# Two reorderings in the feed-forward part of a two-layer trunk: another PSUM bank for one transposition, and the fourth weight set made before the third

## The chip, the cores and the metric

The kernel runs on one core of a Trainium2 chip. Times are microseconds (us) on the device. Before the change three runs gave 1443.37, 1441.01 and 1440.71, so the median is 1441.01. The profiled execution is a fourth one and took 1442.07.

## The reference

The input x has 512 tokens of 1024 features, all in float32. Two layers each do this:

- `h = x + W_out( sigmoid(gA) * PoolMixer(u) + sigmoid(gB) * DiffAttn(q, k, v) )`, where one projection of `RMSNorm(x)` gives u, q, k, v, gA and gB
- `x' = h + (silu(gate) * up) @ w_ffn_out`, where `gate, up = split(RMSNorm(h) @ w_ffn_in)`, each 2816 wide

The change touches the feed-forward part: the transposition of `RMSNorm(h)` (and of the next layer's `RMSNorm(x)`), and the weights of `w_ffn_in`.

## The kernel before

**Precision.** Every matrix product in float32 is made of three passes in fp32r. Each operand is split in a rounded part (`hi`) and the rest (`lo`), and TensorE adds `hi*hi`, `hi*lo` and `lo*hi` in PSUM. `split` (lines 195, 196) makes `hi` with a ScalarE cast and `lo` with a VectorE subtraction. `parts` has a second way for weights that lie in DRAM as they are (lines 233 to 235): ScalarE casts `hi`, ScalarE writes the negated rounded value into `lo`, and a DMA issued by GpSimd adds the float32 weights from DRAM onto it. So `lo` is ready when that DMA has landed.

**Norm and transposition.** 512 tokens are 4 tiles of 128 (t = 0 to 3). `normed` scales a tile by its norm (VectorE, line 336) and later, in `turn`, TensorE transposes it: eight transposes of 128x128 (line 300), four into each of two PSUM tiles named `tr`. There are two `tr` buffers, one bank each. The result is read out by `split` for the next layer's input, or by `Quarters.put` for the feed-forward part. For t of 2 and 3, `put` makes sums and differences with the tile of two tokens before (VectorE, lines 389, 390, 395, 398) and splits each of them; both halves of a token are read until line 395. The bank `oy` holds the sums of the attention heads and isn't used outside attention.

**The feed-forward input projection.** Hidden columns are done in pairs of 128-column blocks (`Ffn`, f0 = 0, 2, 4 up to 20: eleven pairs a layer). A pair's gate and up weights and the two halves of the features make a 2x2 block product, which is done with seven products in place of eight. A product is 24 matmuls of 128x256 (`pair_product`, lines 291, 293, 294). It needs a set of weights: sets 1, 2 and 4 are weights as they are and take the DMA way, sets 3, 5, 6 and 7 are sums or differences that VectorE makes from raw weights (lines 774 to 776 and 785) and take the VectorE way. TensorE takes the products in the order 1, 6, 5, 2, 7, 3, 4; the fourth one goes into a `tr` tile. Between the products VectorE adds partial results (lines 816, 824, 830, 836): line 816 reads the accumulator of the sixth product, and the seventh product accumulates onto it and so comes after it.

**Buffers and order.** The split weights stand in six buffers for `hi` (`whi`) and six for `lo` (`wlo`), taken in turn: a set that is made sixth after another takes its buffer, and must wait for the last matmul that reads it. The raw weights have seven buffers, loaded by DMAs that SP issues. Each engine does its instructions in a fixed order that a scheduler writes when the program is built: it goes by the order of the program and by its own forecast of when each operand is there. `tc.issue_after(x)` makes what is traced in its block, on the engine of x, come after x.

In a layer the first two pairs (`early`, f0 = 0 and 2) are begun while the tokens are still normed; their `sums()` is called without `a12` and makes sets 6, 4, 5, 7, 3 in this order. Each later pair calls `sums(True)`, in which the sets are made in the order 1, 6, 5, 2, 7, 3, 4.

Of the kernel before, what the change touches and what calls it, by code (L numbers as in the profile page):

```python
# [13 lines left out]
AF = mybir.ActivationFunctionType  # L14
# [8 lines left out]
NT = S // P  # L23
# [84 lines left out]
def trunk_kernel(  # L108
# [12 lines left out]
    nc = tc.nc  # L121
# [10 lines left out]
    def tr_ps():  # L132
        return ps.tile([P, 512], F32, name="tr", tag="tr", bufs=2)

    oy = ps.tile([P, 2, VD], F32, name="oy", tag="oy")
# [12 lines left out]
    scale = const.tile([P, L * KD + KD], F32, name="scale")  # L148
# [40 lines left out]
    plan = weight_plan()  # L189
    at = [0]  # L190
    transfers = []

    def split(hi, lo, src):

        ins = nc.scalar.copy(hi, src)  # L195
        nc.vector.tensor_sub(lo, src, hi.bitcast(F32))  # L196
        return ins
# [17 lines left out]
    def loaded():  # L215

        i = at[0]
        at[0] += 1
        raw = sb.tile([P, 4, VD], F32, name="raw", tag="raw", bufs=RAWS)
        nc.sync.dma_start(raw.rearrange("p a b -> p (a b)"), wts[i])  # L220
        return i, raw

    def tiles(x):
        return [x[:, k, :] for k in range(x.shape[1])]

    def parts(src, piece_no=None):

        hi = sb.tile([P, 4, VD], F32R, name="whi", tag="whi", bufs=SPLITS)
        lo = sb.tile([P, 4, VD], F32R, name="wlo", tag="wlo", bufs=SPLITS)
        if piece_no is None:  # L230
            split(hi, lo, src)
        else:
            nc.scalar.copy(hi, src)
            nc.scalar.activation(lo, src, AF.Copy, scale=-1.0)  # L234
            nc.gpsimd.dma_start(lo.rearrange("p a b -> p (a b)"), wts[piece_no], accum_op=ALU.add)  # L235
        return tiles(hi), tiles(lo)

# [22 lines left out]
    def later(delay, what):  # L260
        heapq.heappush(waiting, (clock[0] + delay, count[0], what))
        count[0] += 1
# [36 lines left out]
    def transpose(dst, src):  # L299
        nc.tensor.transpose(dst, src, ident)  # L300
        clock[0] += 2 * P

    def rsqrt_mean(ss, n, width, times=(1.0,), eps=None):

        r = sb.tile([P, width], F32, name="r", tag="r", bufs=4)
        part = width // len(times)
        for i, f in enumerate(times):
            cs = slice(i * part, (i + 1) * part)
            e = EPS / (f * f) if eps is None else eps[i]
            nc.vector.tensor_scalar(r[:, cs], ss[:, cs], 1.0 / (n * f * f), e, op0=ALU.mult, op1=ALU.add)  # L310
        nc.gpsimd.tensor_tensor(r, r, mhalf[:, :width], op=ALU.pow)  # L311
        return r

    def small(name, width=1):
        return sb.tile([P, width], F32, name=name, tag=name, bufs=4)
# [12 lines left out]
    def normed(key, t, xh, xl, g, into=None):  # L328

        xs = sb.tile([P, D], F32, name="xs", tag="mj", bufs=2)  # L330
        ss = small("ss")
        nc.scalar.activation(xs, res[t], AF.Square, accum_out=ss)
        r = rsqrt_mean(ss, D, 1)
        for half in range(2):
            cs = slice(half * 512, (half + 1) * 512)
            nc.vector.scalar_tensor_tensor(xs[:, cs], res[t][:, cs], r, g[half], op0=ALU.mult, op1=ALU.mult)  # L336

        def turn():
            tvs = []
            for half in range(2):  # L340
                tp = tr_ps()
                for i in range(4):
                    k = half * 4 + i
                    transpose(tp[:, i * P:(i + 1) * P], xs[:, k * P:(k + 1) * P])
                tv = tp.rearrange("p (k c) -> p k c", k=4)
                tvs.append(tv)
                if into is None:
                    ks = slice(half * 4, half * 4 + 4)
                    copied = split(xh[:, ks, t * P:(t + 1) * P], xl[:, ks, t * P:(t + 1) * P], tv)
            if into is not None:  # L350
                copied = into(t, tvs)
            ready.add((key, t))
            return copied

        later(NORM_WAIT, turn)
# [158 lines left out]
    for layer in range(L):  # L514
# [197 lines left out]
        def add_out(pairs, t, cb, parts=1, store=False):  # L712
            n = 512 // parts
            for i in range(parts):
                here = mm_ps()[:, :n]
                product(here, [(a, (b[0][:, i * n:(i + 1) * n], b[1][:, i * n:(i + 1) * n])) for a, b in pairs])
                cs = slice(cb * 512 + i * n, cb * 512 + (i + 1) * n)
                added = nc.vector.tensor_add(res[t][:, cs], here, res[t][:, cs])  # L718
                if store:
                    nc.sync.dma_start(out[token(t), cs], res[t][:, cs])  # L720
            return added
# [13 lines left out]
        def hidden_pair(f0):  # L735
            tag = HIDDEN_AT[f0]
            if tag in ("u", "m", "mj"):
                hh, hl = (sb.tile([P, 2, S], F32R, name="f" + part, tag=tag, bufs=2) for part in "hl")
                return [(hh[:, i, :], hl[:, i, :]) for i in range(2)]
            tags = (("pr0", 2), ("pr1", 2)) if tag == "pr" else (("up", 2), ("us", 2))  # L740
            out = []
            for tg, bufs in tags:
                out.append([sb.tile([P, S], F32R, name="f" + part, tag=tg, bufs=bufs) for part in "hl"])
            return out

        class Ffn:
# [12 lines left out]
            def gate(self, k, piece_no=None):  # L759
                self.sets[1 + k] = parts(self.r12 if k else self.r11, piece_no)  # L760
# [4 lines left out]
            def sums(self, a12=False):  # L765

                _, r21 = loaded()
                n22, r22 = loaded()
                if a12:
                    self.gate_raw(1)  # L770
                s1 = sb.tile([P, 4, VD], F32, name="ws", tag="raw", bufs=RAWS)
                if a12:
                    self.gate(0, self.n11)
                nc.vector.tensor_add(s1, r21, r22)
                nc.vector.tensor_sub(r21, self.r11, r21)
                nc.vector.tensor_sub(self.r11, s1, self.r11)
                self.sets[6] = parts(self.r11)
                if not a12:
                    self.sets[4] = parts(r22, n22)
                self.sets[5] = parts(s1)  # L780
                if a12:
                    self.gate(1, self.n12)
                else:
                    self.sets[7] = parts(r21)
                nc.vector.tensor_sub(self.r12, self.r12, self.r11)
                if a12:
                    self.sets[7] = parts(r21)
                self.sets[3] = parts(self.r12)
                if a12:
                    self.sets[4] = parts(r22, n22)  # L790
                self.to = hidden_pair(self.f0)
                for i in range(2):
                    hidden[self.f0 + i] = self.to[i]
# [189 lines left out]
```

## Time and profile before

| what | value |
|---|---|
| median of three runs | 1441.01 us |
| profiled execution | 1442.07 us, with a span of 1440.3 us from its first to its last instruction |
| TensorE (PE) busy | 1431.5 us, 99% of the span |
| VectorE (DVE), ScalarE (ACT), GpSimd (POOL) busy | 991.1, 689.1, 115.1 us |
| granted TensorE clock | 1.000 over the whole span |

PE is busy nearly throughout, so what can change is the sum of its few stops and what each of them is waiting for. The profile models the end of a matmul, so that consecutive ones overlap on paper: how long a group takes is read from the start of its first matmul to the start of what follows it.

### The profile page before, as it was taken

The numbers are of one execution on the slowest core, as the hardware profiler recorded it, in microseconds if no ns is written. First come the engines' busy times: TensorE is split into PE (matmuls) and PEld (weight loads), VectorE is DVE, ScalarE is ACT, GpSimd is POOL, SyncE is SP. The second block draws the span as 40 slices with busy tenths as digits, with TensorE's granted clock in tenths as the row PEclk, the third lists the DMA queues.
The fourth block names the chain that finished last, engine by engine and source line by source line (L and its number), as shares of the span: only waits on it lengthen the run. The fifth ranks groups of instructions, "written<-read, shape, count | busy, mean of one in ns | idle before, by whom it ended". The sixth has DMA issues, their size and how long they took to land.

```text
span 1440.3 us, 21598 instructions
## 1 busy us (share of the span) xinstructions
PE 1431.5 (99%) x8375; PEld 1261.0 (88%) x8375; DVE 991.1 (69%) x1841; ACT 689.1 (48%) x1311; POOL 115.1 (8%) x146
## 2 busy tenths in 40 slices
PE   9999999999999999999999999999999999999999
PEld 6878888888999889989888888888889998999897
DVE  7767677677898548737676685675769975587462
ACT  6544353444667337526355443434546662464350
POOL 1010000000011001001010101001000110010000
PEclk9999999999999999999999999999999999999999
DMA  9311231224258357728322132222332783575361
GB/s 348 109 61 59 96 117 59 89 73 124 66 158 215 117 133 181 200 44 227 124 88 81 59 114 73 85 73 74 114 77 74 188 218 106 130 190 164 78 157 59
DMA packets 50070, 173.02 MB, mean 120 GB/s; under 512 B 5680, under 2 KB 6576, under 8 KB 49968
## 3 DMA queue, kind: packets, MB, share of 16 engines
q1 hardware_dynamic: 39744, 137.02, 28.5%
q0 software_dynamic: 8928, 32.51, 12.6%
q10 hardware_dynamic: 1296, 2.11, 0.6%
q8 instruction: 66, 1.08, 0.3%
q14 instruction: 36, 0.29, 0.1%
HBM read 169.52 MB, written 2.10 MB: 119 GB/s over the span
## 4 chain that ended last, share of the span: by engine, by line
PE 90%; DVE 4%; issue 3%; DMA 2%; POOL 1%; ACT 0%; SPq 0%; POOLq 0%; ACTq 0%
PE mm L279 19%; PE mm L281 19%; PE mm L280 19%; PE mm L291 5%; PE mm L293 5%; PE mm L294 5%; PE sc L294 2%; PE sc L293 2%; PE sc L291 2%; PE tr L300 2%; PE tr L294 1%; DMA wlo<-in_wts 1%; PE tr L291 1%; PE tr L293 1%; DVE xs L336 1%
## 5 line engine op out<-in xcount | busy, mean ns | idle before, releaser
L195 ACT CAST whi<-raw 128x1024 fp32r<-128x1024 f32 (+1 forms) x223 | 232.2, 1047 | 206.6 <-issue 117.2
L196 DVE TENSOR_TENSOR wlo<-raw,whi 128x1024 fp32r<-128x1024 f32 (+1 forms) x223 | 269.6, 1216 | 78.0 <-ACT whi L195 75.0
L279 PE MATMUL mm<-whi,xh 128*128 128x512 f32 x480 | 192.5, 401 | 0.0
L280 PE MATMUL mm<-wlo,xh 128*128 128x512 f32 x480 | 188.0, 392 | 0.5 <-DVE wlo L196 0.5
L281 PE MATMUL mm<-whi,xl 128*128 128x512 f32 x480 | 187.8, 391 | 0.0
L718 DVE TENSOR_TENSOR res<-mm,res 128x512 f32<-128x512 f32 (+1 forms) x97 | 65.9, 683 | 116.0 <-PE mm L281 115.9
L281 PE MATMUL mm<-whi,fl 128*128 128x512 f32 (+1 forms) x358 | 138.7, 387 | 0.0
L279 PE MATMUL mm<-whi,fh 128*128 128x512 f32 (+1 forms) x358 | 138.4, 387 | 0.0
L280 PE MATMUL mm<-wlo,fh 128*128 128x512 f32 (+1 forms) x358 | 138.3, 387 | 0.0
L311 POOL TENSOR_TENSOR r<-r,mhalf 128x1 f32<-128x1 f32 (+1 forms) x76 | 58.2, 765 | 637.2 <-DVE r L310 574.3
L281 PEld LDWEIGHTS mm<-whi,xl 128*128 128x128 f32 x480 | 90.1, 188 | 19.7 <-issue 0.2
L280 PEld LDWEIGHTS mm<-wlo,xh 128*128 128x128 f32 x480 | 90.5, 188 | 17.3 <-DVE wlo L196 0.8
L279 PEld LDWEIGHTS mm<-whi,xh 128*128 128x128 f32 x480 | 90.3, 188 | 16.8
L235 POOL DMA_DIRECT2D wlo<-in_wts x62 | 54.3, 876 | 614.9 <-ACT wlo L234 263.7
L279 PE MATMUL mm<-xh,whi 128*128 128x512 f32 x256 | 102.1, 399 | 0.0
L281 PE MATMUL mm<-xh,wlo 128*128 128x512 f32 x256 | 100.0, 391 | 0.0
L291 PE MATMUL mm<-xrh,whi 128*128 128x256 f32 x352 | 99.9, 284 | 0.2
L280 PE MATMUL mm<-xl,whi 128*128 128x512 f32 x256 | 99.9, 390 | 0.0
L293 PE MATMUL mm<-xrl,whi 128*128 128x256 f32 x352 | 99.8, 284 | 0.0
L294 PE MATMUL mm<-xrh,wlo 128*128 128x256 f32 x352 | 99.8, 283 | 0.0
L291 PE MATMUL mm<-xqh,whi 128*128 128x256 f32 x352 | 99.8, 283 | 0.0
L293 PE MATMUL mm<-xql,whi 128*128 128x256 f32 x352 | 99.8, 283 | 0.0
(212 smaller groups left out, 3527.8 us busy)
## 6 DMA issues: line engine op xcount, KB each, us to landing
raw<-in_wts SPq DMA_DIRECT2D x243, 512.0 KB, 4.4
wlo<-in_wts POOLq DMA_DIRECT2D x62, 512.0 KB, 7.9
res<-in_x SPq DMA_DIRECT2D x4, 512.0 KB, 8.8
pwr<-in_pool_w ACTq DMA_DIRECT2D x8, 256.0 KB, 2.7
out<-res SPq DMA_DIRECT2D x7, 256.0 KB, 2.0
xr<-in_x_t SPq DMA_DIRECT2D x3, 512.0 KB, 8.3
g<-in_gains SPq DMA_DIRECT2D x6, 256.0 KB, 3.3
xr<-in_x_t SPq DMA_DIRECT2D x2, 256.0 KB, 4.4
```

Of the source, the lines that this page charges most:

```text
L195: ins = nc.scalar.copy(hi, src)
L196: nc.vector.tensor_sub(lo, src, hi.bitcast(F32))
L235: nc.gpsimd.dma_start(lo.rearrange("p a b -> p (a b)"), wts[piece_no], accum_op=ALU.add)
L279: nc.tensor.matmul(acc, lhsT=ah, rhs=bh, start=i == 0, stop=False)
L280: nc.tensor.matmul(acc, lhsT=ah, rhs=bl, start=False, stop=False)
L281: nc.tensor.matmul(acc, lhsT=al, rhs=bh, start=False, stop=i == n - 1)
L291: nc.tensor.matmul(acc[:, i, :], lhsT=ah, rhs=bh, start=start and not i and not k, stop=False, skip_group_check=True)
L293: nc.tensor.matmul(acc[:, i, :], lhsT=ah, rhs=bl, start=False, stop=False, skip_group_check=True)
L294: last = nc.tensor.matmul(acc[:, i, :], lhsT=al, rhs=bh, start=False, stop=i == 1 and k == 3, skip_group_check=True)
L300: nc.tensor.transpose(dst, src, ident)
L311: nc.gpsimd.tensor_tensor(r, r, mhalf[:, :width], op=ALU.pow)
L718: added = nc.vector.tensor_add(res[t][:, cs], here, res[t][:, cs])
```

## The change

The transposition of the last token tile (t = 3) puts its first half into the bank `oy` and only its second half into a `tr` tile; this holds for both norms that go through `turn`. In the pairs with `a12`, set 4 is made before set 3. In all pairs the ScalarE cast of set 3 is ordered behind the latest negating copy of `parts` (line 234).

```diff
+    negated = []
...
-            nc.scalar.activation(lo, src, AF.Copy, scale=-1.0)
+            negated[:] = [nc.scalar.activation(lo, src, AF.Copy, scale=-1.0)]
             nc.gpsimd.dma_start(lo.rearrange("p a b -> p (a b)"), wts[piece_no], accum_op=ALU.add)
...
-                tp = tr_ps()
+                tp = oy.rearrange("p a b -> p (a b)") if t == NT - 1 and not half else tr_ps()
...
                 if a12:
                     self.sets[7] = parts(r21)
-                self.sets[3] = parts(self.r12)
-                if a12:
                     self.sets[4] = parts(r22, n22)
+                with tc.issue_after(negated[-1].ins):
+                    self.sets[3] = parts(self.r12)
```

## Rows read from the trace of the kernel before

**Rows 1.** The page, part 1: busy time, share of the span, instructions.

```profile
PE 1431.5 (99%) x8375; PEld 1261.0 (88%) x8375; DVE 991.1 (69%) x1841; ACT 689.1 (48%) x1311; POOL 115.1 (8%) x146
```

**Rows 2.** PE's waits over the span: us in total, times, longest.

```profile
PE tr L294 <- DMA wlo<-in_wts: 1.2, 2, 0.7
...
PE tr L300 <- DVE xd L395: 0.9, 2, 0.6
...
PE tr L300 <- DVE xl L196: 0.2, 1, 0.2
```

**Rows 3.** PE's timeline (start, us, what), first layer: tiles t = 2, t = 3.

```profile
376.64 1.03 PE L300 MATMUL tr<-ident,xs 128*128 128x128 f32 x8
377.43 0.36 PE L291 MATMUL sc<-xqh,whi 128*128 128x256 f32 x1
...
383.32 0.60 PE L300 MATMUL tr<-ident,xs 128*128 128x128 f32 x4
...
384.90 0.36 PE L291 MATMUL sc<-xqh,wxh 128*128 128x256 f32 x1
```

**Rows 4.** Stretches: length, PE, PEld, DVE, ACT, POOL busy, clock, DMA share, GB/s.

```profile
376.30:396.30 20.00, 19.43 (x161) 19.02 (x159) 19.85 (x31) 13.18 (x21) 1.45 (x2) 1.00 0.44 122
1090.50:1110.50 20.00, 19.68 (x163) 19.22 (x161) 19.85 (x31) 13.23 (x21) 1.47 (x2) 1.00 0.47 124
```

**Rows 5.** Timelines of DVE and PE, first layer, around the sixth and seventh products.

```profile
389.69 0.69 DVE L196 TENSOR_TENSOR xrl<-xd,xrh 128x512 fp32r<-128x512 f32 x1
...
390.49 0.33 PE L293 MATMUL mm<-xrl,whi 128*128 128x256 f32 x1
...
394.43 1.22 DVE L774 TENSOR_TENSOR ws<-raw 128x1024 f32<-128x1024 f32 x1
395.57 0.69 DVE L816 TENSOR_TENSOR cqn<-mm,cqn 128x512 f32<-128x512 f32 x1
...
396.40 0.36 PE L291 MATMUL mm<-xrh,whi 128*128 128x256 f32 x1
```

**Rows 6.** PE's timeline: fourth product and what follows, both layers.

```profile
437.01 0.28 PE L291 MATMUL tr<-xth,whi 128*128 128x256 f32 x1
437.13 0.28 PE L293 MATMUL tr<-xtl,whi 128*128 128x256 f32 x1
438.08 0.39 PE L294 MATMUL tr<-xth,wlo 128*128 128x256 f32 x1 [0.66 <-DMA wlo<-in_wts]
...
440.81 0.28 PE L291 MATMUL sc<-xqh,whi 128*128 128x256 f32 x1
...
1154.82 0.28 PE L291 MATMUL sc<-xqh,whi 128*128 128x256 f32 x1
```

**Rows 7.** Timelines of ACT and POOL around the late transfers, both layers.

```profile
424.88 1.06 ACT L195 CAST whi<-raw 128x1024 fp32r<-128x1024 f32 x1 [1.07 <-DVE raw L785]
...
426.79 1.06 ACT L234 ACTIVATE wlo<-raw 128x1024 fp32r<-128x1024 f32 x1
...
428.20 0.86 POOL L235 DMA_DIRECT2D wlo<-in_wts  x1 [4.52 <-ACT wlo L234]
430.64 0.88 POOL L235 DMA_DIRECT2D wlo<-in_wts  x1 [1.57 <-ACT wlo L234]
...
1144.86 0.87 POOL L235 DMA_DIRECT2D wlo<-in_wts  x1 [1.49 <-ACT wlo L234]
```

**Rows 8.** DMA queues, 428.3:432.3: packets, MB, share of 16 engines.

```profile
q1 hardware_dynamic: 403, 1.46, 100.9%
```

**Rows 9.** Two more stretches, with the columns of rows 4.

```profile
424.00:440.50 16.50, 15.84 (x130) 15.47 (x130) 13.80 (x16) 10.57 (x12) 2.62 (x3) 1.00 0.97 253
1138.50:1154.00 15.50, 14.94 (x124) 14.68 (x123) 13.10 (x16) 10.18 (x11) 2.62 (x3) 1.00 1.03 257
```

**Rows 10.** DMA issues, 430.5:431.5, then 1144.5:1145.5: size, us to landing.

```profile
wlo<-in_wts POOLq DMA_DIRECT2D x1, 512.0 KB, 9.9
...
wlo<-in_wts POOLq DMA_DIRECT2D x1, 512.0 KB, 9.1
```

## The prediction

> **What bounds the kernel now.** I read the page first: PE is busy 1431.5 of 1440.3 us [rows 1], so the kernel is as long as PE's stream of matmuls, and only PE's stops can be won or lost. Next I read PE's list of waits [rows 2]. Three of its entries lie where the change works: two stops in the fourth product of a pair, until the accumulating DMA of its set has landed; two stops among the transposes, until VectorE has read a `tr` tile (line 395, in `put`); and one more among the transposes of the other norm. All five together are 2.3 us of idle time in a span of 1440.3. The other 20 of the 22 fourth products do not stop at all.
>
> A stop costs more than its idle time, since the matmul behind it starts with a longer step, so I price each from start to start. Eight unbroken transposes take 377.43 - 376.64 = 0.79; the last tile's eight take 384.90 - 383.32 = 1.58 [rows 3]. The stop there costs 0.79; 0.6 of it is idle [rows 2], so 0.2 is restart. The second layer's stop of this kind has the other 0.3 of the 0.9 idle and so costs 0.5, and the one of 0.2 at the other norm costs 0.4. For the fourth product: matmuls of a pair start 0.12 apart (437.13 - 437.01), 24 of them take 2.88, and this product took 440.81 - 437.01 = 3.80 [rows 6]. So this stop costs 0.92, of which 0.66 is idle and 0.26 restart. The second layer's has the remaining 0.5 to 0.6 idle of [rows 2], and costs 0.8. The whole of what the change can take away is therefore 0.79 + 0.5 + 0.4 + 0.92 + 0.8 = 3.4 us.
>
> Then I read, for each stop, what is late next: busy time by stretch [rows 4], the timelines around each place [rows 5 to 7], and the DMA queues [rows 8 to 10].
>
> **The change part by part.**
>
> *The last tile's first half goes to `oy`.* No instruction is added; four transposes write another bank. That bank's earlier users are the heads' sums of the same layer, and its next ones those of the next layer, both far from here, so I put no wait on it. The second half finds the `tr` tile that the third token freed first. All three transposition stops go.
>
> Whether this time is kept is another matter. In the 20 us from 376.3 on, VectorE is busy 19.85, and 19.85 again in the same stretch of the second layer [rows 4]. It is the engine that is late there, and the change takes no work off it. The first matmul after the stop that depends on it is the second one of the sixth product: it reads `xrl`, which VectorE finishes at 389.69 + 0.69 = 390.38, and it starts at 390.49 [rows 5]. There is 0.11 of slack. If PE arrives 0.79 earlier, it waits here. The seventh product has no slack at all: it comes after line 816, which ends at 395.57 + 0.69 = 396.26, and it starts right behind it, at 396.40. So with VectorE's order as it is, the 0.79 and 0.5 of the feed-forward norm are worth 0: the transposes end earlier and the seventh product starts when it did. The bounds are 0 and 1.29 gained (VectorE's order lets line 816 come earlier by as much); I take 0, because both layers' stretches are full.
>
> At the other norm, between the layers, PE goes on with projections of tiles that were normed before, and no wait of PE on VectorE's norm stands in [rows 2] beside this one. I take the whole 0.4 as won (bounds 0.2, the idle time alone, and 0.4).
>
> *Set 4 before set 3.* Nothing is added or removed: two ScalarE copies and one GpSimd DMA issue move ahead of one cast and one subtraction. In the pair with the late transfer ScalarE stands idle for 1.07, from 423.81 to 424.88, because the cast of set 3 waits for VectorE's line 785; only then come set 4's cast and negation, until 426.79 + 1.06 = 427.85, and the DMA is issued at 428.20, 0.35 later [rows 7]. With set 4 first, its cast can start at about 423.8. Its buffer is now the one that the previous pair's set 3 used, which PE has left by then. Cast and negation take 1.06 each, so the negation ends at about 425.9 and the DMA is issued at about 426.3, 1.9 earlier.
>
> What is that worth at landing? From its issue to PE's next matmul it took 438.08 - 428.20 = 9.9 [rows 6, 7], and that is not its own length: for the 4 us from 428.3 on the queue of the raw loads (q1) was the only one with packets, at a share of 100.9% [rows 8]. What was issued before it was served before it. Issued 1.9 earlier it has no more ahead of it than before, so with the same 9.9 at most it lands by 436.2; it is wanted at 437.13 + 0.12 = 437.25. I take both fourth-product stops as gone.
>
> What is late next is the transfer behind it, set 1 of the next pair. It was issued at 430.64 and took 9.9, so it landed at 440.5 [rows 7, 10]. PE wants it at the third matmul of the next pair: 440.81 + 0.24 = 441.05 before, 440.13 when the stop of 0.92 is gone [rows 6]. The DMA engines are busy 0.97 of the time from 424 to then [rows 9], and the same bytes are still to be moved, with this one last; so I leave its landing at 440.5. Then a new stop of 0.4 idle and 0.1 to 0.26 restart appears, and the first layer keeps 0.92 - 0.5 = 0.4. In the second layer the same transfer landed 9.1 after its issue at 1144.86, at 1153.96 [rows 7, 10]; it will be wanted at 1154.82 - 0.8 + 0.24 = 1154.26 [rows 6]. That is 0.3 of slack, and the second layer keeps all of its 0.8. Bounds for the two layers together: 0.4 (both moved to another transfer) and 1.72.
>
> The Trainium skill, "DMA: Bandwidth & Descriptors", section "Queues, rings and completion order", says that each DMA engine takes the queue rows that have work in turn, switching at packet boundaries. By that rule the accumulating queue would not have to let 4 us of raw loads pass, as it did in [rows 8]; shared out in turns, set 1 would land before it is wanted in both layers, and the sum below would be 2.1 in place of 1.6.
>
> *The costs elsewhere.* Set 3 is made after set 4, some 2 us later. Its cast and subtraction take 1.06 and 1.22 (operations of this size in [rows 5, 7]), and the third product comes five products or 14.4 us after the pair's first. Set 7 now takes the buffer of the previous pair's set 4, the last that PE reads, in place of set 3's: 2.88 later. It is used four products, 11.5 us, into the pair. Both hide beside products. ScalarE stands behind set 7's cast for up to 2.88, with the next pair's results (line 728) queued behind it, whose readers are a round away. The raw buffer of set 4 comes free earlier, that of set 3 later, by one copy each, and SP's loads follow them. For the two early pairs ScalarE's order stays as it is, since set 4 is ahead of set 3 there anyway. I put 0 for all these; if the cover were gone, a stop would stand in the seventh or third product.
>
> **The sum.** 0 (feed-forward norm) + 0.4 (other norm) + 0.4 + 0.8 (fourth products) = 1.6 us less. Against its own time the profiled execution would go from 1442.07 (span 1440.3 and 1.8 around it) to 1440.5. It was 1.1 above the median of the runs, 1441.01; against that median the time is 1439.4.
>
> **The rivals.**
>
> *All is kept.* The scheduler gets the last tile's data earlier in its own forecast, and may put line 816 ahead of the 1.22 of line 774 that stands right before it [rows 5]; set 1 may also land in time. Then up to 3.4 go: 1437.6. For it: one swap in VectorE's order suffices. Against it: the operations ahead of line 816 come first in the program.
>
> *The stops only move.* Set 4's DMA is not issued early enough, or another transfer of the crowded stretch is late in its place in both layers, and the fourth products give 0 to 0.4. With the other norm's 0.4 this is 1440.4. For it: the DMA engines are full there in both layers [rows 9], so whatever goes ahead pushes something back. Against it: 1.9 earlier is twice the 0.92 that is missing.
>
> *VectorE's order gets worse.* The fixed order is written anew. In the stretch of [rows 4] whole-set operations of 1.22 fill in between the token's own ones (line 774 in [rows 5] is one). Each further one that is put ahead of `xrl` or line 816 holds the sixth or seventh product by 1.22, as there is 0.11 of slack. Two in each layer cost 4.88, less 1.6: 1444.3. It makes the kernel slower from two such operations on, and tells from noise from four on. For it: a full engine and a re-made order. Against it: the change only makes inputs come earlier there.
>
> **Chances.** What a measurement of this kernel can tell from no change is about 0.2%, 2.9 us. My forecast (1438.6 to 1440.2 as its own range) has 0.50, all kept 0.24, stops moved 0.14, worse order 0.09; the rest, 0.03, is what I don't see. Faster by over 0.2% means below 1438.1: most of all kept, 0.21, and the lower edge of the forecast, 0.03, give 0.24. Slower by over 0.2%: 0.10, from the worse order and the unseen. Within: 0.66. The range reaches from all kept with a little noise, 1437.3, to one misplaced operation in each layer, 1439.4 + 2.44 = 1441.8.
>
> **What would show it.** Right: no wait of PE on `wlo` from DMA in a fourth product, and none of line 300 on line 395; the sixth product of the first early pair waits for `xrl` and the seventh for line 816, together about as long as the transposes did before; a small new wait in the first product of the pair after the late one, first layer only. Wrong: line 816 ends as much earlier as the transposes (then the norm's 1.29 is kept), the waits in the fourth product are still there, or new PE waits in third or seventh products of the later pairs.

## The result and the profile after

The change makes the kernel slower, by 0.42%: the median of six runs is 1447.4 us (1445.79 to 1448.51), that of six runs before 1440.93, and the ratio is 1.0042 (95% interval 1.0032 to 1.0053), which is worked out over all runs and so is not the quotient of the two medians. I had put 1439.4, with a range that ended at 1441.8, and gave slower a chance of 0.10. The profiled execution took 1445.79, with a span of 1443.9. Line numbers are one higher than before from the split (now 196 and 197) on: the negation is L235, GpSimd's DMA L236, the raw load L221, the three matmuls of a product L292, L294 and L295.

PE's waits after, as in [rows 2] (us in total, times, longest):

```profile
PE sc L295 <- DMA wlo<-in_wts: 5.0, 2, 2.5
...
PE mm L294 <- DVE xrl L197: 0.9, 2, 0.6
```

All three kinds of stop in [rows 2] are gone. The stop of the feed-forward norm (the h-norm) came back at the sixth product, which now waits 0.9 for `xrl`, as much as the transposes waited before. And there is one I did not expect, nearly four times as long as any that went (2.5 against 0.7): the accumulator is `sc`, so it is not the fourth product but the *second* of a pair, and it waits for its set's accumulating DMA. PE's timeline of the two places (start, us, what, idle before and releaser):

```profile
427.39 0.28 PE L292 MATMUL sc<-xqh,whi 128*128 128x256 f32 x1
427.51 0.28 PE L294 MATMUL sc<-xql,whi 128*128 128x256 f32 x1
430.29 0.39 PE L295 MATMUL sc<-xqh,wlo 128*128 128x256 f32 x1 [2.50 <-DMA wlo<-in_wts]
...
433.02 0.28 PE L292 MATMUL mm<-xrh,whi 128*128 128x256 f32 x1
...
1143.03 0.28 PE L294 MATMUL sc<-xql,whi 128*128 128x256 f32 x1
1145.77 0.58 PE L295 MATMUL sc<-xqh,wlo 128*128 128x256 f32 x1 [2.46 <-DMA wlo<-in_wts]
1146.15 0.41 PE L292 MATMUL sc<-xqh,whi 128*128 128x256 f32 x1
...
1149.86 0.28 PE L292 MATMUL mm<-xrh,whi 128*128 128x256 f32 x1
```

This is set 2 of the pair f0 = 4, the first pair of the ones that call `sums(True)`, once in each layer. From the stop to the next product it took 433.02 - 430.29 = 2.73 in the first layer and 1149.86 - 1145.77 = 4.09 in the second, for the same 22 matmuls. The stretches say why (columns as in [rows 4]):

```profile
376.30:396.30 20.00, 19.36 (x160) 18.98 (x159) 19.85 (x29) 13.01 (x21) 1.46 (x2) 1.00 0.47 132
...
430.30:434.00 3.70, 3.70 (x31) 3.70 (x32) 2.48 (x3) 1.89 (x2) 0.13 (x1) 1.00 1.04 279
1145.50:1149.00 3.50, 3.23 (x15) 3.23 (x16) 2.29 (x3) 1.04 (x1) 0.43 (x1) 0.52 1.03 269
```

The granted clock (the column before the last two) was 1.00 after the first stop and 0.52 over the 3.5 us after the second, most of it at the lower of the two levels, 1.2 in place of 2.4 GHz. In the first stretch VectorE is still busy for 19.85 of 20 us, as it was in [rows 4].

Both traces have the same 8375 matmuls in the same order on PE, so the starts of the same one can be laid side by side:

| matmul | before | after | after - before | step |
|---|---|---|---|---|
| end of the kernel's start | 12.59 | 11.86 | -0.74 | -0.74, first loads, not the change |
| last tile's second half transposed, layer 1 | 384.49 | 382.99 | -1.50 | -0.76 |
| sixth product, second matmul | 390.49 | 389.67 | -0.82 | +0.68 |
| second product, third matmul | 428.52 | 430.29 | +1.77 | +2.59 |
| fourth product, third matmul | 438.08 | 439.02 | +0.94 | -0.83 |
| other norm, last tile | 732.18 | 732.71 | +0.52 | -0.42 |
| last tile, layer 2 | 1098.73 | 1098.76 | +0.03 | -0.49 |
| sixth product | 1104.74 | 1105.20 | +0.46 | +0.43 |
| second product, third matmul | 1142.64 | 1145.77 | +3.14 | +2.68 |
| thirteenth one on, half clock | 1144.29 | 1148.71 | +4.43 | +1.29 |
| fourth product, third matmul | 1152.09 | 1155.86 | +3.78 | -0.65 |
| end of span | 1440.30 | 1443.92 | +3.62 | -0.16 |

The two new stops and the half clock cost 2.59 + 2.68 + 1.29 = 6.56; everything that was meant to go did go, and is worth 0.08 + 0.83 + 0.42 + 0.06 + 0.65 = 2.04, where a norm's gain and what is given back behind it are taken together. A row stands at the first matmul behind a stop, so the end of the longer step behind that stop counts for the next row. Taken from the matmul ahead of a stop to the second one behind it, the first new stop is 2.53, the fourth products are 0.92 and 0.82, the other norm is 0.39, and the h-norm's 0.80 and 0.54 are given back as 0.79 and 0.55.

The two profiled executions differ by 3.7, the medians by 6.5. Of the rest, 1.1 is that the profiled execution before was longer than its median, and 1.6 that the profiled one after is the shortest of its six: the others are 1.2 to 2.7 us longer, and their mean granted clocks lower, 0.996 to 0.998 (0.999 in the profiled one). A second stretch at half clock, as two traces below have it, costs about that much, but the other after runs have no trace that would show it.

Why is set 2 late? The timeline of ScalarE, GpSimd and SP's queue, after:

```profile
420.03 0.70 ACT L196 CAST fh<-th 128x256 fp32r<-128x256 f32 x2
420.64 1.04 ACT L234 CAST whi<-raw 128x1024 fp32r<-128x1024 f32 x1
421.58 1.05 ACT L235 ACTIVATE wlo<-raw 128x1024 fp32r<-128x1024 f32 x1
...
423.00 0.86 POOL L236 DMA_DIRECT2D wlo<-in_wts  x1 [15.14 <-ACT fh L196]
423.03 3.26 SPq L221 DMA_DIRECT2D raw<-in_wts  x3
```

and the same place before, with the matmul that needs the set:

```profile
420.79 0.71 ACT L195 CAST fh<-th 128x256 fp32r<-128x256 f32 x2
421.39 1.06 ACT L234 ACTIVATE wlo<-raw 128x1024 fp32r<-128x1024 f32 x1
...
422.81 0.86 POOL L235 DMA_DIRECT2D wlo<-in_wts  x1 [14.19 <-PE sc L294]
423.79 1.42 SPq L220 DMA_DIRECT2D raw<-in_wts  x2
...
428.27 0.28 PE L293 MATMUL sc<-xql,whi 128*128 128x256 f32 x1
428.52 0.39 PE L294 MATMUL sc<-xqh,wlo 128*128 128x256 f32 x1
```

Before, set 2's negation follows the two casts of `fh`. After, one more cast stands between: 420.64, set 4's. PE runs 0.76 ahead of the trace of before here, and the raw load is issued ahead by that too (423.79 to 423.03); set 2's DMA is issued 0.19 later, so by PE's time 0.95 later. What was issued 0.98 before the raw load is now issued 0.03 before it. The issues' sizes and times to landing, after and then before:

```profile
wlo<-in_wts POOLq DMA_DIRECT2D x1, 512.0 KB, 7.2
raw<-in_wts SPq DMA_DIRECT2D x1, 512.0 KB, 3.9
```

```profile
wlo<-in_wts POOLq DMA_DIRECT2D x1, 512.0 KB, 5.7
raw<-in_wts SPq DMA_DIRECT2D x1, 512.0 KB, 5.9
```

The order of landing has turned round: 428.5 ahead of 429.7 before, 430.2 behind 426.9 after. The queues' packets, with MB and the share of 16 engines, from 423.5 to 426.0 show it, after, then before. q0 is GpSimd's queue, q1 SP's:

```profile
q1 hardware_dynamic: 114, 0.47, 81.3%
```

```profile
q0 software_dynamic: 52, 0.21, 59.6%
```

In this stretch each trace moves one transfer alone, and not the same one. So the stop has two parts: 0.95 from the negation and 7.24 - 5.66 = 1.58 from standing behind the raw load. Together they are the 2.53 of this stop. The second layer has the same parts: its DMA is issued 1.49 later (1138.58 after, 1137.09 before) where PE is 0.53 later, which leaves 0.96, and takes 7.15 in place of 5.50, which is 1.65.

### The profile page after: what moved, and what is told of

It reads as the page before. It is cut to its first block, busy times and chain, and to the rows that moved or that the text cites. A ratio compares the mean times of both kernels' runs of the same rounds, so it can differ in the third digit from the quotient of the medians.

```text
span 1443.9 us, 21595 instructions
## 1 busy us (share of the span) xinstructions
PE 1431.6 (99%) x8375; PEld 1261.9 (87%) x8375; DVE 991.7 (69%) x1841; ACT 690.0 (48%) x1311; POOL 115.3 (8%) x146
## 4 chain that ended last, share of the span: by engine, by line
PE 91%; DVE 4%; issue 3%; DMA 1%; POOL 1%; ACT 0%; POOLq 0%
PE mm L280 19%; PE mm L282 19%; PE mm L281 19%; PE mm L294 5%; PE mm L292 5%; PE mm L295 5%; PE sc L295 2%; PE sc L292 2%; PE sc L294 2%; PE tr L301 2%; PE tr L295 1%; PE tr L294 1%; PE tr L292 1%; DMA wlo<-in_wts 1%; DVE xs L337 1%
## 5 line engine op out<-in xcount | busy, mean ns | idle before, releaser
L236 POOL DMA_DIRECT2D wlo<-in_wts x62 | 54.5, 878 | 612.5 <-DVE wlo L197 240.6
L294 PE MATMUL mm<-xrl,whi 128*128 128x256 f32 x352 | 99.8, 284 | 0.9 <-DVE xrl L197 0.9
L292 PE MATMUL mm<-xrh,whi 128*128 128x256 f32 x352 | 99.7, 283 | 0.1
L292 PE MATMUL mm<-xqh,whi 128*128 128x256 f32 x352 | 99.6, 283 | 0.0
L294 PE MATMUL mm<-xql,whi 128*128 128x256 f32 x352 | 99.6, 283 | 0.0
L295 PE MATMUL mm<-xqh,wlo 128*128 128x256 f32 x352 | 99.6, 283 | 0.0
```

What stands on the lines that cost most here:

```text
L292: nc.tensor.matmul(acc[:, i, :], lhsT=ah, rhs=bh, start=start and not i and not k, stop=False, skip_group_check=True)
L294: nc.tensor.matmul(acc[:, i, :], lhsT=ah, rhs=bl, start=False, stop=False, skip_group_check=True)
L295: last = nc.tensor.matmul(acc[:, i, :], lhsT=al, rhs=bh, start=False, stop=i == 1 and k == 3, skip_group_check=True)
```

## The experiments

The times are medians, with the ratio to the kernel before on the same chip; that one's median was 1441.22 beside the first four and 1441.38 beside the others.

| kernel | us | ratio, 95% | PE's stops at the places in question |
|---|---|---|---|
| the bank alone | 1440.79 | 0.9999 (0.9990 to 1.0008) | fourth products 1.0, `xrl` 0.9 |
| the set order alone | 1447.17 | 1.0041 (1.0028 to 1.0053) | second products 4.9, transposes 0.9 and 0.2 |
| set order, set 4 behind set 2's negation | 1439.56 | 0.9987 (0.9978 to 0.9996) | transposes 0.9 and 0.2 |
| both edits, set 4 behind set 2's negation (the fourth kernel) | 1439.19 | 0.9984 (0.9975 to 0.9993) | `xrl` 0.9 |
| before, set 2's cast made twice | 1447.83 | 1.0037 (1.0025 to 1.0050) | second products 4.8, transposes 0.9 and 0.2 |
| both edits, raw load held back | 1440.89 | 0.9995 (0.9986 to 1.0004) | second products 1.4, `xrl` 0.9 |
| both edits, sets 7 and 4 behind the negation | 1441.83 | 1.0001 (0.9992 to 1.0010) | seventh products 2.5, `xrl` 0.9 |
| the fourth kernel, other order on VectorE | 1439.64 | 0.9988 (0.9979 to 0.9997) | seventh product of f0 = 2, 1.7 |

**Which edit.** The kernel before with the bank edit alone:

```diff
-                tp = tr_ps()
+                tp = oy.rearrange("p a b -> p (a b)") if t == NT - 1 and not half else tr_ps()
```

> The transposition edit alone, the order of the sets as before. My theory (set 2's transfer comes late because set 4's cast was put ahead of set 2's negation on ScalarE): no change of that order here, so no long stop in the second product (at most the 0.2 us of before), the two 1 us stops in the fourth product stay, the transposition stops move to the sixth product (0.6 and 0.3 us idle, waiting for xrl). Time 0.4 us below before, 1440.5. Rival (PE comes to the second product earlier because of the transposition edit, and meets the transfer too early): stops of about 2.5 us in the second product of both layers, 5 to 7 us above before, some 1446.

And with the order of the sets alone (the lines that set `negated` are as in the change):

```diff
...
                 if a12:
                     self.sets[7] = parts(r21)
-                self.sets[3] = parts(self.r12)
-                if a12:
                     self.sets[4] = parts(r22, n22)
+                with tc.issue_after(negated[-1].ins):
+                    self.sets[3] = parts(self.r12)
```

> The order of the sets alone, the transposition as before. My theory: both stops of about 2.5 us in the second product appear, and a stretch of half clock after one or both of them; the fourth-product stops are gone; 5.5 to 7.5 us above before, 1446.5 to 1448.5. Rival (it was the transposition): no such stops, 1.7 us below before, 1439.2.

The bank alone has no new stop, and its difference of 0.43 is the size of the other norm's 0.39, which its trace shows too, though its interval includes no change. The order alone has a loss as large as the whole change's and the second products' stops. Two stretches of its trace fall to the lower clock, from 1.6 and 1.2 us behind the ends of the stops (429.97 and 1147.10) on (columns as in [rows 4]):

```profile
431.50:435.00 3.50, 3.50 (x19) 3.50 (x18) 1.44 (x2) 2.09 (x2) 0.00 (x0) 0.51 1.05 280
1148.30:1151.80 3.50, 3.50 (x19) 3.50 (x18) 1.58 (x2) 1.77 (x2) 0.00 (x0) 0.51 1.05 277
```

In each, PE does 19 matmuls in 3.5 us, where at 0.12 apart it does 29.

**The one cast.** If set 4's cast ahead of set 2's negation is the cause, one line that orders it behind must cure the loss, and leave the fourth products' gain. First without the bank edit, then with it:

```diff
-                    self.sets[4] = parts(r22, n22)
+                    with tc.issue_after(negated[-1].ins):
+                        self.sets[4] = parts(r22, n22)
```

> The order of the sets as changed, the transposition as before, and set 4's cast and negation ordered behind set 2's negation on ScalarE; set 4's transfer still goes out about 2 us after set 2's. My theory: set 2's transfer goes out as before the change, ahead of the raw load, and lands in time: stop in the second product at most 0.3 us, none in the fourth; 1.7 us below before, 1439.2. Rival (set 4's transfer, 2 us behind, takes the DMA engines from set 2's): the stops in the second product stay at 1 to 2.5 us, 1443 to 1447.

> The whole change, with set 4's cast and negation ordered behind set 2's negation. My theory: the stops of the second product go, the transposition of the norm between the layers gives 0.4 more than the order of the sets alone: 2.1 us below before, 1438.8. Rival (set 4's transfer disturbs set 2's): as in the run before it, 1443 to 1447.

The timeline of the fourth kernel, both edits with this line:

```profile
420.88 1.06 ACT L235 ACTIVATE wlo<-raw 128x1024 fp32r<-128x1024 f32 x1
422.09 0.71 ACT L196 CAST fh<-th 128x256 fp32r<-128x256 f32 x2 [0.16 <-DVE th L731]
422.29 0.86 POOL L236 DMA_DIRECT2D wlo<-in_wts  x1 [14.18 <-PE sc L295]
422.71 1.04 ACT L234 CAST whi<-raw 128x1024 fp32r<-128x1024 f32 x1
423.27 1.42 SPq L221 DMA_DIRECT2D raw<-in_wts  x2
```

Set 4's cast now stands behind the negation, at 422.71, and set 2's DMA is 0.98 ahead of the raw load again. Neither the second nor the fourth products stop any more. Both kernels are faster than the one before, and the last is the best version of this study: 2.0 us less than before and 8 less than the change as it was made. Its gain is larger than the 1.6 that I had put on the change, since the new stop in set 1 of the next pair, 0.5 in my sum, did not appear: that set's DMA was issued at 429.79, took 8.9 in place of the 9.9 that I had kept for it, and landed 0.7 before PE wanted it.

**Plain delay or the raw load ahead?** Two readings of the new stop were left: that set 2's DMA is simply later by one cast, 0.95, or that it also loses its place before the raw load. The first test delays the negation by one cast in the kernel *before*, with the order of the sets untouched:

```diff
+            if twice:
+                nc.scalar.copy(hi, src)
...
-                self.sets[1 + k] = parts(self.r12 if k else self.r11, piece_no)
+                self.sets[1 + k] = parts(self.r12 if k else self.r11, piece_no, k == 1 and self.f0 == 4)
```

> The kernel before the change (set 3 ahead of set 4), with one thing added: in the pair with f0 = 4 of each layer ScalarE makes the cast of set 2 twice, so that its negation and its transfer come about 0.95 us later, as they do in the changed kernel; set 4's transfer stays late. My theory (0.95 us on ScalarE lets a raw load go ahead of set 2's transfer on the DMA engines): a stop of 2 to 3 us in the second product of both layers although set 4 is not early; the fourth-product stops fall away behind it; 4 to 8 us above before. Rival (a plain delay without any overtaking): the transfer lands 0.95 us later, so a stop of 1.0 to 1.2 us in each layer, and the fourth product gains back about as much: 0 to 1 us above before.

It is as slow as the change: a stop of 2.4 in each layer. In its timeline the second cast is at 420.86, and the two issues are again 0.03 apart:

```profile
420.86 1.05 ACT L235 CAST whi<-raw 128x1024 fp32r<-128x1024 f32 x1
421.80 1.06 ACT L236 ACTIVATE wlo<-raw 128x1024 fp32r<-128x1024 f32 x1
...
423.22 0.86 POOL L237 DMA_DIRECT2D wlo<-in_wts  x1 [15.14 <-ACT fh L195]
423.25 1.42 SPq L220 DMA_DIRECT2D raw<-in_wts  x2
...
430.41 0.39 PE L296 MATMUL sc<-xqh,wlo 128*128 128x256 f32 x1 [2.40 <-DMA wlo<-in_wts]
```

So a cast's delay is enough, whatever it casts. Nor does it take set 4's own transfer, which the change issues early: here that goes out only at 427.65, and set 2's takes 7.2 all the same. The second test leaves the change as it is and holds the raw load back: VectorE reads one column of `s1`, whose buffer the load overwrites, behind its next subtraction.

```diff
-                nc.vector.tensor_sub(self.r12, self.r12, self.r11)
+                less = nc.vector.tensor_sub(self.r12, self.r12, self.r11)
+                if self.f0 == 4:
+                    with tc.issue_after(less.ins):
+                        nc.vector.tensor_copy(small("sso"), s1[:, 0, :1])
```

> The changed kernel, with one thing added: in the pair with f0 = 4 VectorE reads one column of the buffer that the next raw load fills, about 1.9 us after its last read so far, so that this load is issued behind set 2's transfer and not beside it. ScalarE's order is that of the changed kernel. My theory: set 2's transfer moves at once, takes 5.5 to 6 us and lands some 1.5 us earlier; the stop in the second product shrinks from 2.5 to about 1 us in each layer, and the time from 1447 to about 1443. Rival (its own late issue is the whole cause, or set 4's transfer behind it): the stops stay at 2.5 us, 1447.

The order of the sets is that of the change, and the negation is as late; only the load that was held came later. It is the second of the two in SP's line below, at 425.50; the one at 424.72 was the next one so far and stands where it did, 1.12 behind set 2's DMA:

```profile
423.60 0.86 POOL L236 DMA_DIRECT2D wlo<-in_wts  x1 [15.13 <-ACT fh L196]
...
424.72 1.11 SPq L221 DMA_DIRECT2D raw<-in_wts  x2
...
428.11 0.28 PE L294 MATMUL sc<-xql,whi 128*128 128x256 f32 x1
429.11 0.38 PE L295 MATMUL sc<-xqh,wlo 128*128 128x256 f32 x1 [0.71 <-DMA wlo<-in_wts]
```

The stop fell from 2.50 to 0.71, and the mean granted clock was 1.000. Set 2's transfer took 5.5, near the 5.7 of before, so what is left is the cast's 0.95 less the 0.2 of that difference. The time came out 2 us below my expectation: the trace has no stretch at half clock either, which I had left in. Both readings were thus part of it: about 0.9 of the stop is delay, 1.6 the place behind the load, and the half clock comes on top.

**How far back can sets be moved?** With set 7 ordered behind the negation as well:

```diff
-                    self.sets[7] = parts(r21)
-                    self.sets[4] = parts(r22, n22)
+                    with tc.issue_after(negated[-1].ins):
+                        self.sets[7] = parts(r21)
+                        self.sets[4] = parts(r22, n22)
```

> The whole change, with set 7's and set 4's casts ordered behind set 2's negation, which then comes another 0.95 us earlier than in the kernel before. My theory: the last remains of a stop in the second product (0.1 to 0.2 us) go; otherwise as with set 4's cast alone behind it, 2.1 to 2.4 us below before, 1438.9. Rival (the earlier transfer pushes back the raw load that comes after it, and VectorE's sums wait): new stops in the sixth or seventh product, 1440 or more.

The second products' stop is gone and one in the seventh product has come, of 1.28 in the first layer. ScalarE now has three casts and a negation of whole sets ahead of line 809's copy, and does it at 426.68 (at 423.66 in the fourth kernel). Line 818 reads that copy, and VectorE's fixed order has put it behind line 775, which waits for raw weights:

```profile
429.23 1.23 DVE L775 TENSOR_TENSOR ws<-raw 128x1024 f32<-128x1024 f32 x1 [2.92 <-DMA raw<-in_wts]
430.37 1.22 DVE L197 TENSOR_TENSOR wlo<-raw,whi 128x1024 fp32r<-128x1024 f32 x1
431.51 0.69 DVE L818 TENSOR_TENSOR cqn<-mm,cqn 128x512 f32<-128x512 f32 x1
```

In the fourth kernel the same addition ran at 426.06, ahead of line 775, which ran at 429.15 there: so it is the order that changed, and not a load that came later, as my rival had it. The gain that I expected (1438.9) did not come. The mechanism is that of the prediction's third rival (VectorE's order gets worse), in another pair than I had it in and called up by a late operand.

**Can the h-norm's gain be kept?** The fourth kernel, with the early pairs' work interleaved and the first sum and set 7 of f0 = 2, and set 7 of f0 = 0, held behind `xrl`:

```diff
...
+            sixth[:] = rest
...
-                nc.vector.tensor_add(s1, r21, r22)
+                with ExitStack() as behind:
+                    if self.f0 == 2:
+                        behind.enter_context(tc.issue_after(sixth[-1].ins))
+                    nc.vector.tensor_add(s1, r21, r22)
...
-                    self.sets[7] = parts(r21)
+                    with tc.issue_after(sixth[-1].ins):
+                        self.sets[7] = parts(r21)
...
             for x in early:
                 x.sums()
-            for x in early:
                 x.rest()
```

`sixth` is the subtraction that makes `xrl`.

> The whole change with set 4's cast behind set 2's negation, and VectorE's order in the stretch of the last token changed: set 7's subtraction of the first early pair and the first sum of the second one come after xrl, and line 816 of the first pair ahead of that sum. My theory (VectorE's order alone decides whether the time of the transposition is kept): xrl ends about 1 us earlier, the stops in the sixth and seventh products of the first early pair (0.73 and 0.23, and 0.49 and 0.23 in the second layer) go; 1.7 us below the same kernel without it, 3.7 below before, 1437.4. Rival (PE there waits for something else right behind, a raw load or ScalarE): at most 0.5 us below it.

The wait for `xrl` went, but the second early pair's seventh product waits instead. VectorE's and PE's timeline there:

```profile
408.86 1.22 DVE L198 TENSOR_TENSOR wlo<-raw,whi 128x1024 fp32r<-128x1024 f32 x1
409.99 0.68 DVE L824 TENSOR_TENSOR cqn<-mm,cqn 128x512 f32<-128x512 f32 x1
...
410.73 0.39 PE L293 MATMUL mm<-xrh,whi 128*128 128x256 f32 x1 [0.88 <-DVE cqn L824]
```

Work that was put behind `xrl` is done by VectorE ahead of line 824. The gain is given back within the two early pairs, and the time, 1439.64, is no better than the fourth kernel's, where I had expected 1437.4. VectorE is busy for 27.40 of the 27.70 us from 383.0 to this stop. Whether some other order would keep it was not tried.

## Why the prediction was wrong

**The step that failed** is "Set 4 before set 3. Nothing is added or removed: two ScalarE copies and one GpSimd DMA issue move ahead of one cast and one subtraction", with the start that I gave: "With set 4 first, its cast can start at about 423.8". I looked for set 4's new place in the idle 1.07 that [rows 7] show. The scheduler took an earlier one, 420.64, ahead of set 2's negation: set 4's raw weights were there, and nothing in the changed program held it back. Why the scheduler's forecast preferred this place no trace shows. My list of "the costs elsewhere", put at 0, names sets 3 and 7, the results of the next pair and the raw buffers. Set 2 is not in it.

The trace of before held what was needed. Its matmul at 428.52 starts 0.25 after the one before it, with the longer first step that follows a stop; set 2's transfer landed at 428.47, so this product was already waiting a little, too short to stand in the list of waits. There was less than no slack. And the raw load was issued 0.98 behind it, one ScalarE cast. I had priced the transfers behind set 4, and not the one in front of it.

A second assumption of mine failed with it: "What was issued before it was served before it". After, set 2's DMA was issued first and landed last of the two. The trace of before shows this too, at another place, where GpSimd's DMA is issued at 377.96 and SP's load 0.14 behind it:

```profile
wlo<-in_wts POOLq DMA_DIRECT2D x1, 512.0 KB, 8.2
raw<-in_wts SPq DMA_DIRECT2D x1, 512.0 KB, 3.9
```

**The rivals.** "The stops only move" came nearest, since a transfer of the crowded stretch became late. But I bounded it by the gain that would be lost, and not by what a transfer out of its place costs. "VectorE's order gets worse" had the right cause, a fixed order that is written anew, on the wrong engine; it was the only case of mine that ended slower by enough to tell.

**The order of the two queues.** The rows here show one transfer first and the other behind it: 114 packets of one queue and none of the other, and in the trace before 52 of the other queue and none of this one. The Trainium skill, "DMA: Bandwidth & Descriptors", section "Queues, rings and completion order", says that an engine changes between rows of queues at packet boundaries. I had read that as sharing the 4 us of [rows 8] in small turns, which these rows do not show. The Trainium skill gives in the same section 9 to 17 descriptors as typical of a packet. A raw load has 144 of the profile's packets over 16 engines (423 to 427 after), 9 an engine. If the packet of the rule is what such a load puts on one engine, the rule says what the rows show. No run here tells more.

**Right:** the h-norm's gain is worth nothing, at the place and in the size that I gave ([rows 5]: `xrl`; 0.80 won and 0.79 given back, in the second layer 0.54 and 0.55), though all of it is given back at the sixth product and the seventh does not wait; the other norm's 0.4 (0.39); both fourth-product stops go (0.92 and 0.82 for 0.92 and 0.8). **Mis-sized:** the new stop of 0.5 in set 1 of the next pair. It did not show after, where PE is later, nor in the third and fourth kernels, where it is not: I had kept the transfer's 9.9, and it took 8.9 there. What made it shorter no run isolates. With set 2 kept in its place, the change gives the 1.6 that I forecast and a little more: 2.0.

## What to carry to other kernels

When work is moved ahead on an engine with a fixed order, list what it can now stand before, up to the earliest time its operands are there, and not only the gap in which you would like it; then write down, for every transfer that these operations release, the slack at its reader and the distance to the next issue on any other queue. A transfer issued just ahead of another can fall behind it, so a delay of one cast, 0.95, cost 2.5 here. If a set must go first, pin it behind the operation that releases the nearest deadline: one line turned 0.4% slower into 0.16% faster here.

## What the hardware showed that I had not expected

GpSimd's accumulating DMA and SP's load do not keep their order when issued together: at 0.03 us apart the later of the two landed 3.3 us earlier (426.9 against 430.2), at 0.98 apart the earlier one landed first. The packets suggest why. SP's load has its first packet 0.96 after its issue (423.99 after), GpSimd's transfer 1.57 (424.38 before); and in the change GpSimd's packets start only at 426.19, when the load's are nearly done. So the order should turn where the issues are about 0.6 apart, an estimate from these two delays. Other places of the traces lie on either side: at 0.14 (377.96 before) the load landed first, at 0.88 (458.60 after) GpSimd's transfer. No run tests a distance near 0.6 with these two transfers alone.

A stop of 2.5 us can cost more than itself. Behind it the granted clock fell to 0.5 for some 3.4 us in both layers of two traces and in one layer of the change's own, and each such stretch cost 1.3 to 1.5; behind the other stop of the change's own, as long, it stayed at 1.00, and so it did behind stops of 0.7. A kernel with such stops shows it as scatter: the six runs of the change lie within 2.7 us, the longer ones at the lower mean clock, and the eleven of the fourth kernel, all at 1.000, within 1.3. One run of the kernel with the cast made twice had a mean clock of 1.000; it took 1444.56, where the median there is 1447.83.
